# A list scheduler learns that VectorE and ScalarE wait on the result of their direct predecessor

## The chip, the cores and the metric

One core of a Trainium2 chip runs the whole program. The metric is device time in microseconds of one execution. The kernel before the change takes 1433.64 us, the median of three runs (1433.3 to 1433.87). Engines are called by their names in the profile: PE is TensorE's matmul row and PEld its weight loads, DVE is VectorE, ACT is ScalarE, POOL is GpSimd, SP is the queue on which most transfers are issued.

## The reference

Two layers over a sequence of 512 positions, width 1024, all in float32.

- Layer 0: RMSNorm, one input projection, a gated linear recurrence and trailing means, an output projection, residual.
- Layer 1: RMSNorm, a projection of twice the width with a sigmoid gate, a causal convolution of 31 taps per channel, LayerNorm over the channels, swish, a second projection, residual.
- After each: cross-attention with 4 heads into 256 memory tokens, and a gated MLP of inner width 3072 with a causal convolution of 3 taps on its gate branch.

```python
def conformer_conv(x, norm, w1, b1, dw_w, dw_b, ln_g, ln_b, w2, b2):
    h = rms_norm(x, norm) @ w1 + b1
    h = jax.nn.glu(h, axis=-1)
    h = causal_dwconv(h, dw_w, dw_b)
    h = jax.nn.silu(layer_norm(h, ln_g, ln_b))
    return h @ w2 + b2
...
def conv_ffn(x, norm, w_up, dw_w, dw_b, w_down):
    h = rms_norm(x, norm) @ w_up
    g = causal_dwconv(h[..., :D_FF], dw_w, dw_b)
    u = h[..., D_FF:]
    return (jax.nn.gelu(g) * u) @ w_down
```

## The kernel before the change

Channels lie on partitions in tiles of 128, positions along the free dimension. Every float32 operand of a matmul is split into a rounded high half and a low half (`split`: ACT copies the high half, DVE, in places POOL, subtracts it for the low half), and three matmuls stand for one product (`mm3`: high x high, high x low, low x high). Weights come by DMA as `wf` tiles and are split into pairs of `wr` tiles. So each weight costs ACT and DVE one pass each.

Nothing is issued where it is written. A class `Recorder` takes down every operation as a `Node`, then `plan` simulates the five engines and issues the operations in the order of that simulation. All instructions carry the line of the issuing statement in `run` (L498), so places are told by tiles here.

- `cost` gives each node a duration, and `lat`, the time after it until another engine sees its result (PE 0.17, ACT 0.1, DVE 0.08, POOL 0.06 us). `HOP` is 0.04 us on top.
- `late` walks the nodes backwards and gives each a due time, from the due times of its successors.
- The loop in `plan` then picks, on each engine that is free, the ready operation with the smallest rank: the recorded index on PE (within a window of 60 PE nodes), the due time elsewhere. A node becomes ready at `hop(a)` after its last predecessor: for one on the same engine, as soon as the predecessor's duration is over.
- Buffers of the tags `act` and `w` are given out by due time, the others in recorded order.

The chip runs each engine's list strictly in that order, and semaphores see to correctness. Where the simulation believes an engine to be earlier than it is, the real list holds an operation too early, and what stands behind it waits.

Three stages matter below. **The MLP** (`ffn`): per chunk of 128 inner channels, `up` makes seven products of eight matmuls into three PSUM tiles, x in `aux`, w and y in `mm`. ACT copies x out three times and w once (`copy`, tiles `tmp`), and the next product into that tile must wait for the copy. Between the products stand 24 matmuls of `down` for the group before, which have no such wait and serve as cover. **The convolution** (`conformer`): for each of 8 channel tiles, `gated` writes h with one DVE operation, four transfers stack shifted copies of h (tiles `actf`, read by `conv_pe`), PE does the first 8 taps (all taps of the last tile) as matmuls of 32 columns, POOL with ACT does 4, and DVE adds the other 19 one by one into PSUM. **The end of it**: LayerNorm over all eight tiles, then the second projection with weights `pw2`.

## Time and profile before

| | before |
|---|---|
| median of 3 runs | 1433.64 us |
| profiled execution | 1433.83 us |
| its span, first to last instruction | 1432.0 us |
| PE busy | 1421.8 us (99%) |
| weight loads (PEld) | 1199.9 us (84%) |
| DVE busy | 1223.8 us (85%), 1874 instructions |
| ACT busy | 853.2 us (60%) |
| POOL busy | 185.3 us (13%) |
| granted TensorE clock | 1.000 |

The profiled execution takes 1.83 us outside its span, and lies 0.19 us over the median. A row of the timeline gives the start, the duration, engine, line, operation, the tiles written and read, the shape, how many instructions were merged into the row, and in brackets how long the engine had been idle before and what ended that. A row of waits gives an engine and its tile, what it waited for, the total, the count and the longest. Matmul ends are modelled, so a short wait of PE can hide in a busy row.

### The profile page before, as it was taken

The page shows a single profiled execution, that of the slowest core. Times are in us where ns is not written, and L with a number is a line of the kernel's source. Part 1 is how long each engine was busy: PE and PEld are TensorE (multiplying, and loading weights), DVE is VectorE, ACT ScalarE, POOL GpSimd, SP SyncE. Part 2 cuts the span into 40 slices and gives each one's busy share as a digit, 9 for nine tenths or more (in the row PEclk, how much of TensorE's full clock was granted, in tenths as well). Part 3 has the DMA queues.
Part 4 walks back from the last instruction along what each step waited for, and adds up shares of the span by engine and source line. Part 5 has one row for each costly group of instructions (what it writes and reads, how often), then busy time and mean ns, then how long its engine had stood idle before and what let it go on. Part 6 is the DMA issues. An engine that isn't in the chain of part 4 may idle for free. (4 is left out here: it accounts for less than half of the span.)

```text
span 1432.0 us, 20240 instructions
## 1 busy us (share of the span) xinstructions
PE 1421.8 (99%) x7512; PEld 1199.9 (84%) x7512; DVE 1223.8 (85%) x1874; ACT 853.2 (60%) x1298; POOL 185.3 (13%) x196
## 2 busy tenths in 40 slices
PE   9999999999999999999999999999999999999998
PEld 8888888888988888888886676888898888888888
DVE  8986964758999999999967996776699999999996
ACT  8578854446866566656643436654577665666654
POOL 0000000001111010110006663300011111011000
PEclk9999999999999999999999999999999999999999
DMA  9332322228877786886515572322688777787821
GB/s 349 104 103 74 123 96 90 76 86 224 234 205 209 208 215 188 216 211 178 166 57 136 134 230 75 118 84 79 175 230 213 205 192 221 205 222 181 216 90 60
DMA packets 75988, 231.91 MB, mean 162 GB/s; under 512 B 8561, under 2 KB 10609, under 8 KB 75889
## 3 DMA queue, kind: packets, MB, share of 16 engines
q1 hardware_dynamic: 61488, 192.20, 40.7%
q0 software_dynamic: 13824, 37.75, 15.6%
q8 instruction: 59, 0.97, 0.3%
q10 hardware_dynamic: 576, 0.67, 0.1%
q14 instruction: 41, 0.33, 0.1%
HBM read 207.52 MB, written 2.10 MB: 146 GB/s over the span
## 5 line engine op out<-in xcount | busy, mean ns | idle before, releaser
L498 PE MATMUL mm<-act,wr 128*128 128x512 f32 (+1 forms) x4599 | 987.3, 368 | 1.7 <-ACT tmp L498 1.0
L498 PEld LDWEIGHTS mm<-act,wr 128*128 128x128 f32 x4599 | 802.1, 188 | 155.2 <-issue 5.8
L498 ACT ACTIVATE wr<-wf 128x1024 fp32r<-128x1024 f32 x295 | 308.4, 1053 | 116.8 <-PE mm L498 27.0
L498 DVE TENSOR_TENSOR wr<-wf,wr 128x1024 fp32r<-128x1024 f32 x272 | 329.4, 1219 | 37.3 <-ACT wr L498 18.7
L498 PE MATMUL aux<-act,wr 128*128 128x512 f32 (+1 forms) x1509 | 293.7, 337 | 0.1
L498 PEld LDWEIGHTS aux<-act,wr 128*128 128x128 f32 x1509 | 232.6, 190 | 28.8 <-ACT tmp L498 0.5
L498 ACT ACTIVATE tmp<-aux 128x512 f32<-128x512 f32 (+1 forms) x189 | 107.5, 571 | 94.8 <-PE aux L498 93.6
L498 DVE TENSOR_TENSOR tmp<-tmp,tmp 128x512 f32<-128x512 f32 (+1 forms) x151 | 99.4, 658 | 10.1 <-ACT tmp L498 6.3
L498 POOL DMA_DIRECT2D wf<-in_wup x48 | 42.7, 889 | 500.9 <-ACT act L498 275.9
L498 DVE TENSOR_TENSOR x<-x,mm 128x512 f32<-128x512 f32 (+1 forms) x126 | 81.5, 648 | 22.3 <-PE mm L498 21.6
L498 DVE SCALAR_TENSOR_TENSOR aux<-h,par,aux 128x497 f32<-128x497 f32 (+18 forms) x133 | 93.1, 731 | 4.7 <-PE aux L498 2.1
L498 POOL DMA_DIRECT2D wf<-wf x48 | 41.5, 864 | 382.0 <-PE mm L498 129.7
L498 ACT ACTIVATE act<-tmp 128x512 fp32r<-128x512 f32 (+1 forms) x85 | 52.9, 627 | 59.5 <-DVE tmp L498 59.4
L498 ACT ACTIVATE act<-actf 128x512 fp32r<-128x512 f32 (+1 forms) x136 | 70.0, 536 | 28.4 <-DVE actf L498 26.4
L498 PE MATMUL aux<-act,act 128*128 128x256 f32 (+1 forms) x456 | 84.4, 327 | 0.0
L498 PEld LDWEIGHTS aux<-act,act 128*128 128x128 f32 x456 | 73.7, 189 | 11.4 <-ACT tmp L498 0.5
L498 DVE TENSOR_TENSOR act<-actf,act 128x512 fp32r<-128x512 f32 (+1 forms) x136 | 76.0, 583 | 1.7 <-ACT act L498 1.5
L498 DVE SCALAR_TENSOR_TENSOR tmp<-h,par,tmp 128x512 f32<-128x512 f32 x96 | 72.0, 750 | 5.3 <-ACT tmp L498 2.7
L498 ACT ACTIVATE tmp<-h,par 128x512 f32<-128x512 f32 (+3 forms) x69 | 52.6, 782 | 31.2 <-DVE h L498 30.9
L498 POOL TENSOR_TENSOR wr<-wf,wr 128x1024 fp32r<-128x1024 f32 x23 | 55.1, 2406 | 91.2 <-PE mm L498 42.2
L498 DVE TENSOR_TENSOR tmp<-mm,tmp 128x512 f32<-128x512 f32 x84 | 57.1, 685 | 6.4 <-PE mm L498 6.1
L498 DVE TENSOR_TENSOR act<-tmp,act 128x512 fp32r<-128x512 f32 (+1 forms) x85 | 57.6, 682 | 0.4 <-ACT act L498 0.2
(150 smaller groups left out, 1067.2 us busy)
## 6 DMA issues: line engine op xcount, KB each, us to landing
wf<-in_wup SPq DMA_DIRECT2D x144, 512.0 KB, 4.8
wf<-in_wup POOLq DMA_DIRECT2D x48, 512.0 KB, 5.7
wf<-in_wdown SPq DMA_DIRECT2D x48, 512.0 KB, 5.3
actf<-in_wup SPq DMA_DIRECT2D x48, 256.0 KB, 6.3
wf<-wf POOLq DMA_DIRECT2D x48, 256.0 KB, 6.0
wf<-in_pw SPq DMA_DIRECT2D x24, 512.0 KB, 4.0
wf<-in_win SPq DMA_DIRECT2D x20, 512.0 KB, 3.6
wf<-in_wk SPq DMA_DIRECT2D x16, 512.0 KB, 5.9
```

The costliest lines, as they stand in the source:

```text
L498: getattr(eng, method)(*[real(a) for a in args], **{k: real(v) for k, v in how.items()})
```

## The change

The scheduler gets a table `DRAIN` with 0.12 us for DVE and 0.2 us for ACT, and each node a set `feeds`: the later nodes that read what it wrote.

- In the forward simulation, a successor on the same engine that reads the result becomes ready `DRAIN` after the predecessor's duration. Another operation may be put in between. A successor that only overwrites is ready as before.
- In `late`, any successor on the same engine now counts with `DRAIN` and no longer with `HOP` and `lat`. For DVE these are equal (0.04 + 0.08 against 0.12), for ACT 0.14 becomes 0.2, for POOL 0.1 becomes 0, and for PE 0.21 becomes 0. So the due times before a chain of matmuls move too.

No operation is added or removed, except that ACT loads an activation table 32 times and no longer 31. Every operation may be issued at another place. In the two programs' lists, a DVE instruction reads what the DVE instruction just before it wrote 370 times before and 120 times after; among the convolution's taps 73 and 29 times. On ACT it is 24 and 13 times.

```diff
--- before.py
+++ after.py
@@ -185,7 +185,7 @@
     def __init__(self, index, eng):
         self.index, self.eng, self.calls, self.us, self.tail = index, eng, [], 0.0, 0.0
         self.table, self.port, self.lat = None, False, 0.0
-        self.before, self.after = set(), set()
+        self.before, self.after, self.feeds = set(), set(), set()
         self.start = self.end = None
 
 
@@ -206,6 +206,7 @@
     PATIENCE = 40.0
     WIRE = 0.83 / (256 * 1024)
     LAND = {"SP": 1.9, "ACT": 1.9, "POOL": 2.3}
+    DRAIN = {"DVE": 0.12, "ACT": 0.2}
 
     def __init__(self, tc):
         self.tc, self.nc = tc, tc.nc
@@ -260,6 +261,8 @@
         for e in t.writes + (t.reads if write else []):
             if meets(e) and e[3] is not node:
                 node.before.add(e[3])
+                if not write:
+                    e[3].feeds.add(node)
         if write:
             keep = lambda e: not (lo <= e[0] and e[1] <= hi and (e[2] & mask) == e[2])
             t.writes = [e for e in t.writes if keep(e)]
@@ -340,7 +343,10 @@
             for o in reversed(nodes):
                 due = end if o.ideal is None else o.ideal + o.us
                 for a in list(o.after) + extra.get(o, []):
-                    due = min(due, a.due - self.HOP - o.lat - (o.tail + self.LAND[o.eng] + self.SAFE if o.tail else 0.0))
+                    if a.eng == o.eng and not o.tail:
+                        due = min(due, a.due - self.DRAIN.get(o.eng, 0.0))
+                    else:
+                        due = min(due, a.due - self.HOP - o.lat - (o.tail + self.LAND[o.eng] + self.SAFE if o.tail else 0.0))
                 o.due = due - 1.15 * o.us
 
         def turn(t):
@@ -451,7 +457,9 @@
                     del r[i]
                     done += 1
                     heapq.heappush(soon, (o.end, o.index, "end", o))
-                    hop = lambda a: now + us if a.eng == o.eng and not o.tail else o.end + self.HOP
+                    drain = self.DRAIN.get(o.eng, 0.0)
+                    same = lambda a: now + us + (drain if a in o.feeds else 0.0)
+                    hop = lambda a: same(a) if a.eng == o.eng and not o.tail else o.end + self.HOP
                     for a, at in [(a, hop(a)) for a in o.after] + [(a, now) for a in opens.get(o, [])]:
                         wait[a] -= 1
                         a.at = max(getattr(a, "at", 0.0), at)
```

Three places, as the programs hold them. A name such as `tmp_1018_5193` is the kernel's tile `tmp_1018` (the same tile in both) and a number of the build, which says nothing. Before is the fence with L498, the change the one with L506.

ACT in an MLP chunk of layer 0, around the copy of `mm_1015` (the chunk's w, `tmp_1018`). `tmp_1019` is a copy of x, `wr_1052` the high half of a weight of a later `down`, `act_1039` and `act_1066` of later `up` weights, `act_995` of the chunk before's result:

```order
L498 ACTIVATE tmp_1017_5160<-aux_1014_5137 128x512
L498 ACTIVATE act_1039_5162<-actf_1032_5099 128x512
L498 ACTIVATE wr_1052_5172<-wf_1051_5077 128x1024
L498 ACTIVATE act_1066_5179<-actf_1059_5127 128x512
L498 ACTIVATE tmp_1018_5193<-mm_1015_5174 128x512
L498 ACTIVATE tmp_1019_5205<-aux_1014_5137 128x512
L498 ACTIVATE act_1093_5221<-actf_1086_5142 128x512
```

```order
L506 ACTIVATE tmp_1017_5153<-aux_1014_5131 128x512
L506 ACTIVATE act_995_5156<-tmp_994_5090 128x512
L506 ACTIVATE wr_1037_5166<-wf_1030_5016 128x1024
L506 ACTIVATE act_1066_5179<-actf_1059_5118 128x512
L506 ACTIVATE tmp_1018_5186<-mm_1015_5168 128x512
L506 ACTIVATE tmp_1019_5198<-aux_1014_5131 128x512
L506 ACTIVATE wr_1052_5222<-wf_1051_5136 128x1024
```

The split `wr_1052` has moved behind both copies, and `act_995` and `wr_1037`, which were ahead of `tmp_1017`, come behind it.

ACT a chunk earlier, at the copies of `mm_988` and of x (`aux_987`):

```order
L498 ACTIVATE tmp_991_5037<-mm_988_5018 128x512
L498 ACTIVATE tmp_992_5053<-aux_987_4987 128x512
L498 ACTIVATE tmp_993_5079<-aux_987_4987 128x512
L498 ACTIVATE tmp_994_5084<-h2_116,par_129 128x512
L498 ACTIVATE wr_1033_5092<-wf_1031_5045 128x1024
```

```order
L506 ACTIVATE tmp_991_5034<-mm_988_5018 128x512
L506 ACTIVATE wr_1025_5043<-wf_1024_4971 128x1024
L506 ACTIVATE tmp_992_5051<-aux_987_4987 128x512
L506 ACTIVATE wr_1035_5080<-wf_1029_4911 128x1024
L506 ACTIVATE tmp_993_5085<-aux_987_4987 128x512
```

The weight splits `wr_1025` and `wr_1035` have moved ahead of the second and the third copy. On PE three matmuls of `down` (into `mm_1000`) now stand ahead of the product that follows the second copy. The lists show this PE pattern at eight chunks.

DVE in the convolution. `aux_1448` and `aux_1467` are the accumulators of the channel tiles 0 and 1, rows into them are taps, and `h2_116` is the h of channel tile 2:

```order
L498 SCALAR_TENSOR_TENSOR aux_1448_7435<-h0_112,par_129,aux_1448_7435 128x483
L498 SCALAR_TENSOR_TENSOR aux_1448_7435<-h0_112,par_129,aux_1448_7435 128x482
L498 SCALAR_TENSOR_TENSOR aux_1467_7545<-h1_114,par_129,aux_1467_7545 128x500
L498 SCALAR_TENSOR_TENSOR aux_1467_7545<-h1_114,par_129,aux_1467_7545 128x499
L498 SCALAR_TENSOR_TENSOR h2_116<-mm_1468_7514,par_129,tmp_1465_7518 128x512
L498 SCALAR_TENSOR_TENSOR aux_1467_7545<-h1_114,par_129,aux_1467_7545 128x498
L498 SCALAR_TENSOR_TENSOR aux_1467_7545<-h1_114,par_129,aux_1467_7545 128x497
L498 SCALAR_TENSOR_TENSOR aux_1467_7545<-h1_114,par_129,aux_1467_7545 128x496
```

```order
L506 SCALAR_TENSOR_TENSOR aux_1448_7441<-h0_112,par_129,aux_1448_7441 128x488
L506 SCALAR_TENSOR_TENSOR aux_1467_7522<-h1_114,par_129,aux_1467_7522 128x499
L506 SCALAR_TENSOR_TENSOR aux_1448_7441<-h0_112,par_129,aux_1448_7441 128x487
L506 SCALAR_TENSOR_TENSOR aux_1467_7522<-h1_114,par_129,aux_1467_7522 128x498
L506 SCALAR_TENSOR_TENSOR aux_1448_7441<-h0_112,par_129,aux_1448_7441 128x486
L506 SCALAR_TENSOR_TENSOR h2_116<-mm_1468_7507,par_129,tmp_1465_7516 128x512
L506 SCALAR_TENSOR_TENSOR aux_1448_7441<-h0_112,par_129,aux_1448_7441 128x485
L506 SCALAR_TENSOR_TENSOR aux_1467_7522<-h1_114,par_129,aux_1467_7522 128x497
```

Taps of two accumulators now alternate, and the write of `h2_116` has three operations fewer ahead of it since the first tap. The write of channel tile 1's h now stands ahead of all taps. On PE, 6 of the matmuls into `mm_1449` and of those into `mm_1487` move from behind the convolution of channel tile 0 and of tile 2 to ahead of it; of those into `mm_1468`, 12 move the other way at tile 1. Ahead of the tile 4 convolution stand 9 matmuls more, ahead of that of tile 6 another 27 (21 of them 256 wide). At the end of the stage, DVE subtracts the low halves of all three first `pw2` weights (`wr_1672`, `wr_1675`, `wr_1678`) ahead of the second activation's (`act_1632`), which before came behind the first.

## The prediction

> **What bounds the kernel now.** I read the page's busy times first, then the chain of waits, then windows of the long stages, then PE's own waits, then the timeline at the places where it waits.
>
> ```profile
> span 1432.0 us, 20240 instructions
> PE 1421.8 (99%) x7512; PEld 1199.9 (84%) x7512; DVE 1223.8 (85%) x1874; ACT 853.2 (60%) x1298; POOL 185.3 (13%) x196
> ```
>
> PE is busy in all but 10 us. A modelled busy time may hide waits, so I look at its pace. In the chain of waits (start, duration, what):
>
> ```profile
> 1243.86 4.11 PE mm L498 x18
> ...
> 1259.10 4.11 PE mm L498 x18
> ...
> 1274.34 4.11 PE mm L498 x18
> ```
>
> A matmul of 512 columns takes 4.11/18 = 0.228 us, and one MLP chunk follows the other in 15.24 us, twice the same. In the chain itself stands nothing but PE. A faster DVE shortens such a chunk by nothing. Windows of two MLP stretches and of the convolution (PE, PEld, DVE, ACT, POOL busy, clock, DMA):
>
> ```profile
> 480.00:520.00 40.00, 39.94 (x208) 33.91 (x207) 39.19 (x58) 22.40 (x32) 4.90 (x6) 1.00 0.78 214
> 760.00:800.00 40.00, 38.76 (x182) 26.98 (x175) 37.30 (x53) 14.75 (x20) 25.27 (x20) 1.00 0.53 142
> 1200.00:1240.00 40.00, 39.52 (x211) 33.72 (x210) 39.02 (x58) 24.26 (x35) 5.05 (x6) 1.00 0.78 204
> ```
>
> DVE runs at 93 to 98% there, so PE's operands come out of it with little to spare. What can be won is what PE waits. Its waits, of matmuls and of weight loads (total, times, longest):
>
> ```profile
> PE aux L498 <- DMA actf<-h: 1.6, 3, 1.0
> PE mm L498 <- ACT tmp L498: 1.0, 2, 0.5
> PE mm L498 <- DVE act L498: 0.6, 1, 0.6
> ...
> PEld aux L498 <- DMA actf<-h: 5.2, 5, 1.9
> PEld mm L498 <- ACT tmp L498: 4.3, 9, 0.9
> PEld mm L498 <- DVE act L498: 1.2, 2, 0.9
> ```
>
> Two causes stand out: the stacked copies of h in the convolution, and ACT's copies of PSUM in the MLP.
>
> **The price of a dependent neighbour.** Timeline of DVE in the convolution:
>
> ```profile
> 764.33 6.13 DVE L498 SCALAR_TENSOR_TENSOR aux<-h,par,aux 128x497 f32<-128x497 f32 x8
> ...
> 793.36 3.90 DVE L498 SCALAR_TENSOR_TENSOR aux<-h,par,aux 128x484 f32<-128x484 f32 x6
> ```
>
> The first row is eight taps into one accumulator, each reading the one before. At 0.74 us for one, the starts lie (6.13 - 0.74)/7 = 0.77 us apart. The second is six taps that alternate between two accumulators: (3.90 - 0.74)/5 = 0.63. So an operation between two that depend saves 0.14 us. The change puts 0.12. With 370 such neighbours before and 120 after, DVE is relieved of 250 x 0.12 to 250 x 0.14, 30 to 35 us of its 1224. [...]
>
> That relief lies beside PE and is worth nothing by itself. It pays where PE waits.
>
> **Term 1, the convolution.** Timeline of PE, each convolution block (32-column matmuls) and the row that follows it:
>
> ```profile
> 759.14 2.28 PE L498 MATMUL aux<-actf,wf 128*32 128x512 f32 x16
> 761.35 11.19 PE L498 MATMUL mm<-act,wr 128*128 128x512 f32 x48
> 772.47 1.92 PE L498 MATMUL aux<-actf,wf 128*32 128x512 f32 x16
> 774.32 9.86 PE L498 MATMUL mm<-act,wr 128*128 128x512 f32 x42
> 784.10 1.16 PE L498 MATMUL aux<-actf,wf 128*32 128x512 f32 x4
> ...
> 789.38 12.54 PE L498 MATMUL mm<-act,wr 128*128 128x512 f32 x54
> ...
> 814.84 1.06 PE L498 MATMUL aux<-actf,wf 128*32 128x512 f32 x6
> ...
> 818.06 9.83 PE L498 MATMUL mm<-act,wr 128*128 128x512 f32 x42
> ...
> 843.01 2.74 PE L498 MATMUL aux<-actf,wf 128*32 128x512 f32 x16
> 845.68 12.53 PE L498 MATMUL mm<-act,wr 128*128 128x512 f32 x54
> ```
>
> The block of channel tile 1 takes 774.32 - 772.47 = 1.85 us and waits for nothing. Tile 0 takes 2.21, tile 2 5.28, tile 4 3.22, tile 6 2.67. Over 1.85 that is 0.36 + 3.43 + 1.37 + 0.82 = 5.98 us, all of it late copies of h. For tile 2 the cause is on DVE:
>
> ```profile
> 763.66 0.74 DVE L498 SCALAR_TENSOR_TENSOR h<-mm,par,tmp 128x512 f32<-128x512 f32 x1
> ...
> 777.89 0.75 DVE L498 SCALAR_TENSOR_TENSOR h<-mm,par,tmp 128x512 f32<-128x512 f32 x1
> ...
> 778.67 4.26 SPq L498 DMA_DIRECT2D actf<-h  x4
> ```
>
> The product it reads was done six matmuls (1.37 us) after 774.32, at 775.7; DVE came to it 2.2 us later, behind taps. In the new list h comes after 19 operations, 12 of which depend on their neighbour: 0.67 + 12 x 0.77 + 6 x 0.63 = 13.7 us after the first, so near 775.2, and then waits for PE. With 0.3 us from PE's end to DVE's start it can be written 1.9 us earlier. PE also runs six more matmuls, 1.37 us, ahead of the block. Of 3.43 us that takes 1.9 + 1.37 = 3.3. For tiles 0, 4 and 6, PE has 6, 9 and 27 matmuls more ahead of the block: 1.37, 2.05 and at least 3 us, more than the 0.36, 1.37 and 0.82 they wait. Only tile 1 loses: its block comes 12 - 6 = 6 matmuls (1.37) earlier, less the 0.36 saved at tile 0. Its h goes ahead of three taps, 763.66 against 761.46 or so, 2.2 us earlier. Between 0 and 0.9 us could be lost, by what the SP queue does; I take 0.4. Together -(0.36 + 3.3 + 1.37 + 0.82) + 0.4 = -5.4, and I take **-5.0**, since tile 2's transfers took 4.26 us to issue and may again. The bounds are 0 (the transfers alone set it) and -5.98. DVE must follow: 44 fewer dependent taps at 0.14 are 6.2 us, enough.
>
> **Term 2, ACT's copies in the MLP.** Timeline around the longest such wait:
>
> ```profile
> 524.08 1.06 ACT L498 ACTIVATE wr<-wf 128x1024 fp32r<-128x1024 f32 x1 [0.29 <-DVE wr L498]
> ...
> 525.57 0.58 ACT L498 ACTIVATE tmp<-mm 128x512 f32<-128x512 f32 x1
> ...
> 526.20 1.48 PEld L498 LDWEIGHTS mm<-act,wr 128*128 128x128 f32 x8 [0.91 <-ACT tmp L498]
> 526.20 1.69 PE L498 MATMUL mm<-act,wr 128*128 128x512 f32 x8 [0.48 <-ACT tmp L498]
> ```
>
> PE waits for the copy of w; ahead of it ACT split a weight for 1.06 us. The loss is more than the 0.48 shown, since a matmul's row is longer than its pace:
>
> ```profile
> L498 PE MATMUL mm<-act,wr 128*128 128x512 f32 x3639 | 876.9, 391 | 1.7 <-ACT tmp L498 1.0 <-DVE act L498 0.6
> ```
>
> 0.391 - 0.228 = 0.16 is hidden, so 0.64 is lost, 0.27 less than the weight load's 0.91. For the nine such waits: 4.3 - 9 x 0.27 = 1.9 us. In the new list the weight split has gone behind both copies, which takes away 1.06 us where 0.64 was missing. Such a split, needed only much later, was early because ACT was thought idle while DVE ran late. I take **-1.6** of 1.9; bounds 0 and -1.9.
>
> **Term 3, new waits.** Two rows of the lists speak for some. At eight chunks a weight split has moved ahead of a copy of x. Ahead of the second projection, DVE subtracts two more weights before the second activation. The wait already there (0.6 on PE, 0.9 on PEld, both by DVE act) may grow: two splits of 1.2 us go ahead, of which three matmuls each (0.68) cover half, so at most about 1 us more. The other side is that this wait goes, -0.8. I take **+1.3** in all, bounds -0.8 and +2.9 (1 plus as much again as the MLP waits now, 1.9). The additional table load lies on ACT, 60% busy, in a mixer without a PE wait; it counts as nothing, and as its 1.28 us, if it fell in a copy's way:
>
> ```profile
> 1.67 1.28 ACT L498 ACT_TABLE_LOAD   x1 [1.67 <-PEq L1591]
> ```
>
> Sum against the profiled execution: 1433.83 - 5.0 - 1.6 + 1.3 = 1428.5, and the median of the runs lies 0.2 lower. I forecast **1428.4 us**. A measurement here tells from no change what is over 0.2%, 2.9 us, so it counts as faster below 1430.8 and as slower above 1436.5.
>
> **Rivals.**
>
> (a) *The copies of h stay late.* The wait is named as DMA, and the issues of these copies (shortest, median and longest in ns) held one of 2.6 us:
>
> ```profile
> L498 SPq DMA_DIRECT2D actf<-h x28: 548/604/2644, 764.5 to 851.2; - x28
> ```
>
> If the queue sets it, earlier h buys nothing: 1433.8 - 1.6 + 1.3 = 1433.5. Against it: PE also comes later to four of the blocks, whatever the queue does.
>
> (b) *Slower: cover spent too early.* At the eight chunks PE now uses three matmuls (0.68 us) ahead of the product after ACT's second copy of x, because the plan puts a split of
>
> ```profile
> L498 ACT ACTIVATE wr<-wf 128x1024 fp32r<-128x1024 f32 x295 | 308.4, 1053 | 116.8 <-PE mm L498 27.0
> ```
>
> 1.05 us ahead of that copy. If ACT reaches the split late, say behind a DVE result, PE pays up to 1.05 at each: 1428.4 + 8 x 1.05 = 1436.8. It outweighs the gains of 5.3 from 0.66 us a chunk on. For it: ACT waits for DVE often. Against it: ACT is 22 to 24 of 40 us busy here, and the new plan counts the delays on DVE that made ACT late.
>
> (c) *DVE is the bound.* If the stretches at 97% DVE are paced by DVE, 30 us of relief come back whole: 1433.8 - 30 = 1404. Against it: two chunks of exactly 15.24 us, and 0.228 us for each matmul. "Perfetto Trace Analysis" of the Trainium skill, in "Identifying the Most-Contended Engine", would point here: it takes weight-load busy, not matmul busy, as PE's measure, and 84% stands below DVE's 85%. The steady pace disagrees.
>
> (d) *It doesn't do what it says.* The price of a dependent neighbour is not saved, the order moves to no end: about 1433.8. The 0.14 us above are against it.
>
> **Chances.** Forecast 0.61, (a) 0.24, (b) 0.10, (c) 0.02, (d) 0.03. Low end: all of term 1, term 2 and the 0.8 of the wait at the second projection gone, with no new wait, 1433.6 - 6.0 - 1.9 - 0.8 = 1424.9. High end: (a) with the worse half of term 3, 1433.5 + 1 = 1434.5. That leaves out (b) and (c). Faster: the forecast and (c), 0.63, and a bit of (a), 0.02: 0.65. Slower is (b) at its full price, or at half of it together with (a), 1433.5 + 4.2 = 1437.7: 0.10. The rest, 0.25, is the same.
>
> **What would show it.** Term 1: the blocks of tiles 2 and 4 at 1.85 to 2.3 us, the wait for DMA actf<-h on PEld under 1.5 us in all, the row of alternating taps for more than half of the taps. Term 2: PEld's wait for ACT tmp in mm under 2 us. DVE's busy time falls by some 25 to 30 us, as neighbours overlap that did not. Term 3: the wait before the second projection at 0.6 to 1.6 us. If PE waits at eight chunks for ACT tmp after 500 us, (b) was right. If tile 2's block still takes over 4 us, (a). The prediction is wrong at its root if PE's 0.228 us or the 15.24 us a chunk change.

## The result

| | before | after |
|---|---|---|
| median of 6 runs | 1433.46 us (1433.05 to 1433.87) | 1423.87 us (1423.04 to 1425.68) |
| profiled execution | 1433.83 us | 1424.79 us |
| its span | 1432.0 us | 1423.0 us |

The ratio is 0.9934, with a 95% interval of 0.9922 to 0.9947. The change saves 9.6 us, nearly twice the 5.2 us that were forecast, and ends 1 us below the low end of the range. The direction was right, the size was not.

The page of the changed kernel, span and busy times:

```profile
span 1423.0 us, 20230 instructions
...
PE 1414.1 (99%) x7512; PEld 1200.0 (84%) x7512; DVE 1204.5 (85%) x1874; ACT 846.6 (59%) x1299; POOL 185.2 (13%) x196
```

DVE has lost 19.3 us of busy time, PE 7.7, and the span 9.0. The change needs the same 7512 matmuls; what it needs less is waiting. PE's timeline (start, duration) at the convolution blocks of the channel tiles 2 and 4, where before lost most:

```profile
782.55 1.92 PE L506 MATMUL aux<-actf,wf 128*32 128x512 f32 x16
...
810.58 1.92 PE L506 MATMUL aux<-actf,wf 128*32 128x512 f32 x16
```

Both, like those of tiles 0, 1, 3 and 6, are a single row of 16 matmuls with the 1.92 us that the undisturbed tile 1 had before (a start-to-start time of 1.85). Tile 5's row shows 1.89 us, as before. The rows with a bracket for DMA actf<-h are gone: the 5.98 us of the blocks have come back in full. DVE's timeline before, at the stage's first taps and its last merge, and after:

```profile
761.46 2.30 DVE L498 SCALAR_TENSOR_TENSOR aux<-h,par,aux 128x500 f32<-128x500 f32 x3 [2.15 <-PE aux L498]
...
865.63 0.75 DVE L498 SCALAR_TENSOR_TENSOR actf<-aux,par,actf 128x512 f32<-128x512 f32 x1
```

```profile
841.22 9.65 DVE L506 SCALAR_TENSOR_TENSOR aux<-h,par,aux 128x500 f32<-128x500 f32 x15 [0.47 <-PE aux L506]
...
860.30 0.75 DVE L506 SCALAR_TENSOR_TENSOR actf<-aux,par,actf 128x512 f32<-128x512 f32 x1
```

The merge comes 5.33 us earlier. Of this, 1.55 us is a first tap that comes earlier (759.91 against 761.46), and 3.8 us is less time between the two. The first row of the second fence is fifteen taps in a row of alternating accumulators, (9.65 - 0.74)/14 = 0.64 us apart.

The prediction showed three rows of the weight loads' waits (5.2, 4.3 and 1.2). The view of before holds more; without its rows named "issue" and three of 0.3 to 0.4 by DVE, these are:

```profile
PEld aux L498 <- ACT tmp L498: 1.4, 6, 0.4
...
PEld stat L498 <- POOL onesf L573: 1.0, 1, 1.0
PEld mm L498 <- ACT wr L498: 0.8, 1, 0.8
...
PEld aux L498 <- POOL actf L498: 0.7, 2, 0.4
PEld aux L498 <- DVE tmp L498: 0.5, 2, 0.3
```

And the same view after, without "issue" and two rows of 0.4:

```profile
PEld aux L506 <- ACT tmp L506: 1.7, 2, 1.3
PEld aux L506 <- DVE wr L506: 1.3, 1, 1.3
PEld stat L506 <- POOL onesf L581: 1.0, 1, 1.0
PEld mm L506 <- DVE act L506: 0.9, 2, 0.5
```

With all rows but "issue" they add up to 16.1 us before and 5.7 after. The difference of 10.4 us is close to the 9.0 of the span. The rows for DMA actf<-h and for mm <- ACT tmp, 9.5 us, are gone. Two waits are new. The first stands before the second projection (PE's timeline):

```profile
885.88 1.64 PE L506 MATMUL mm<-act,wr 128*128 128x512 f32 x5 [0.19 <-DVE act L506]
...
888.86 0.50 PE L506 MATMUL aux<-act,wr 128*128 128x512 f32 x1 [0.88 <-DVE wr L506]
```

Together 1.07 us where 0.60 stood before. The second was not forecast. It lies in the second MLP's first chunks; ACT's timeline there:

```profile
1051.33 0.63 ACT L506 ACTIVATE act<-actf 128x512 fp32r<-128x512 f32 x1 [1.55 <-DMA actf<-in_wup]
1051.86 1.04 ACT L506 ACTIVATE wr<-wf 128x1024 fp32r<-128x1024 f32 x1
1052.81 0.36 ACT L506 ACTIVATE tmp<-aux 128x256 f32<-128x256 f32 x1
```

ACT waits 1.55 us for a weight to land, and the copy that PE needs stands behind this weight's split and another. PE waits 1.03 us, the weight load 1.34.

Where the 9 us were won shows at rows that stand at the same place of both programs: a row late in the first cross-attention, the first row behind the first MLP, the first behind the second projection, and the start of the output. PE's timeline before, and after:

```profile
317.24 1.03 PE L498 MATMUL aux<-ident,tmp 128*128 128x128 f32 x8
...
725.39 5.92 PE L498 MATMUL mm<-wr,act 128*128 128x256 f32 x48
...
944.44 0.62 PE L498 MATMUL stat<-act,ones 128*128 128x512 f32 x2
...
1423.49 0.71 PE L498 MATMUL aux<-ident,actf 128*128 128x128 f32 x5
```

```profile
316.73 1.04 PE L506 MATMUL aux<-ident,tmp 128*128 128x128 f32 x8
...
722.82 5.92 PE L506 MATMUL mm<-wr,act 128*128 128x256 f32 x48
...
936.44 0.62 PE L506 MATMUL stat<-act,ones 128*128 128x512 f32 x2
...
1414.55 0.71 PE L506 MATMUL aux<-ident,actf 128*128 128x128 f32 x5
```

Ahead of the first MLP 0.5 us are won, in the stretch with the first MLP 2.06, in the one with the convolution and the second projection 5.43, and from there on 0.94, all of it in the second MLP.

### The profile page after: what moved, and what is told of

Same layout as the page of the kernel before. It is cut to its first block, busy times and chain, and to the rows that moved or that the text cites. A ratio compares the mean times of both kernels' runs of the same rounds, so it can differ in the third digit from the quotient of the medians.

```text
span 1423.0 us, 20230 instructions
## 1 busy us (share of the span) xinstructions
PE 1414.1 (99%) x7512; PEld 1200.0 (84%) x7512; DVE 1204.5 (85%) x1874; ACT 846.6 (59%) x1299; POOL 185.2 (13%) x196
## 4 chain that ended last, share of the span: by engine, by line
PE 98%; DMA 1%; DVE 0%; ACT 0%; issue 0%; DVEq 0%; POOL 0%; POOLq 0%
PE mm L506 70%; PE aux L506 27%; PE stat L506 1%; DMA actf<-in_wup 1%; DVE wr L506 0%; ACT wr L506 0%; DVE wf L506 0%; DVEq L1607 0%; ACT act L506 0%; ACT tmp L506 0%; ACT rtok L506 0%; DVE rtok L506 0%; POOL onesf L581 0%; POOL eps L581 0%; DVE act L506 0%
## 5 line engine op out<-in xcount | busy, mean ns | idle before, releaser
L506 PE MATMUL mm<-act,wr 128*128 128x512 f32 (+1 forms) x4599 | 988.0, 368 | 0.2 <-DVE act L506 0.2
L506 PEld LDWEIGHTS mm<-act,wr 128*128 128x128 f32 x4599 | 801.4, 188 | 149.8 <-issue 5.5
L506 ACT ACTIVATE wr<-wf 128x1024 fp32r<-128x1024 f32 x295 | 307.3, 1053 | 105.6 <-PE mm L506 34.8
L506 DVE TENSOR_TENSOR wr<-wf,wr 128x1024 fp32r<-128x1024 f32 x272 | 330.8, 1218 | 39.3 <-ACT wr L506 19.8
L506 PE MATMUL aux<-act,wr 128*128 128x512 f32 (+1 forms) x1509 | 293.6, 336 | 1.9 <-ACT tmp L506 1.0
L506 PEld LDWEIGHTS aux<-act,wr 128*128 128x128 f32 x1509 | 234.0, 190 | 30.6 <-ACT tmp L506 1.3
L506 ACT ACTIVATE tmp<-aux 128x512 f32<-128x512 f32 (+1 forms) x189 | 108.0, 572 | 94.3 <-PE aux L506 91.9
L506 DVE TENSOR_TENSOR tmp<-tmp,tmp 128x512 f32<-128x512 f32 (+1 forms) x151 | 97.8, 647 | 11.6 <-ACT tmp L506 11.0
L506 POOL DMA_DIRECT2D wf<-in_wup x48 | 41.9, 872 | 464.8 <-DMA actf<-in_wup 181.2
L506 DVE TENSOR_TENSOR x<-x,mm 128x512 f32<-128x512 f32 (+1 forms) x126 | 81.4, 646 | 20.6 <-PE mm L506 19.9
L506 POOL DMA_DIRECT2D wf<-wf x48 | 41.3, 861 | 410.4 <-DMA wf<-in_wup 127.0
L506 DVE SCALAR_TENSOR_TENSOR aux<-h,par,aux 128x500 f32<-128x500 f32 (+16 forms) x133 | 89.2, 728 | 3.4 <-PE aux L506 2.3
L506 ACT ACTIVATE act<-tmp 128x512 fp32r<-128x512 f32 (+1 forms) x85 | 52.7, 625 | 58.0 <-DVE tmp L506 57.9
L506 ACT ACTIVATE act<-actf 128x512 fp32r<-128x512 f32 (+1 forms) x136 | 68.8, 534 | 26.7 <-DVE actf L506 19.5
L506 PE MATMUL aux<-act,act 128*128 128x256 f32 (+1 forms) x456 | 84.2, 327 | 0.0
L506 PEld LDWEIGHTS aux<-act,act 128*128 128x128 f32 x456 | 73.8, 189 | 10.9
L506 DVE TENSOR_TENSOR act<-actf,act 128x512 fp32r<-128x512 f32 (+1 forms) x136 | 75.4, 580 | 3.2 <-ACT act L506 3.1
L506 DVE SCALAR_TENSOR_TENSOR tmp<-h,par,tmp 128x512 f32<-128x512 f32 x96 | 71.6, 746 | 0.8 <-ACT tmp L506 0.6
L506 DVE TENSOR_TENSOR tmp<-mm,tmp 128x512 f32<-128x512 f32 x84 | 57.2, 686 | 15.9 <-PE mm L506 15.0
L506 POOL TENSOR_TENSOR wr<-wf,wr 128x1024 fp32r<-128x1024 f32 x23 | 55.2, 2408 | 96.2 <-PE mm L506 53.8
L506 ACT ACTIVATE tmp<-mm 128x512 f32<-128x512 f32 (+1 forms) x58 | 33.3, 574 | 55.7 <-PE mm L506 55.6
L506 ACT ACTIVATE tmp<-h,par 128x512 f32<-128x512 f32 (+3 forms) x69 | 52.4, 778 | 18.0 <-DVE h L506 17.9
```

Source lines behind the costliest of these rows:

```text
L506: getattr(eng, method)(*[real(a) for a in args], **{k: real(v) for k, v in how.items()})
```

## The experiments

All in one view first. The neighbours are the dependent ones of DVE in the program's list; the weight load's waits are the sum of all rows of that view but those named "issue"; DVE busy and span are of the profiled execution.

| kernel | neighbours | PEld waits | DVE busy | span | median | ratio to before, interval |
|---|---|---|---|---|---|---|
| before | 370 | 16.1 | 1223.8 | 1432.0 | 1433.5 | 1 |
| the change | 120 | 5.7 | 1204.5 | 1423.0 | 1423.87 | 0.9934, 0.9922 to 0.9947 |
| forward half alone | 140 | 5.9 | 1205.7 | 1422.5 | 1424.70 | 0.9938, 0.9923 to 0.9953 |
| due times alone | 383 | 13.9 | 1224.7 | 1431.2 | 1433.05 | 0.9998, 0.9989 to 1.0008 |
| VectorE's number alone | 121 | 4.3 | 1206.1 | 1421.8 | 1423.70 | 0.9930, 0.9914 to 0.9947 |
| delay counted, gap not filled | 349 | 8.3 | 1222.2 | 1428.9 | 1429.71 | 0.9976, 0.9966 to 0.9985 |
| convolution alone | 331 | 12.6 | 1219.3 | 1427.2 | 1428.88 | 0.9968, 0.9956 to 0.9980 |
| MLPs alone | 223 | 11.4 | 1212.2 | 1427.5 | 1429.12 | 0.9970, 0.9959 to 0.9981 |
| copies of h counted longer | 372 | 17.7 | 1223.2 | 1432.0 | 1433.75 | 1.0001, 0.9992 to 1.0010 |
| before, a tap less | 385 | 16.8 | 1222.3 | 1434.9 | 1436.05 | 1.0017, 1.0008 to 1.0027 |
| delay counted, a tap less | 350 | 6.0 | 1215.9 | 1423.2 | 1425.15 | 0.9944, 0.9927 to 0.9960 |
| the change, a tap more | 117 | 7.1 | 1211.2 | 1425.7 | 1429.03 | 0.9967, 0.9954 to 0.9980 |
| a third of the numbers | 141 | 3.2 | 1205.7 | 1420.9 | 1422.75 | 0.9925, 0.9909 to 0.9942 |
| a third, VectorE alone | 146 | 4.2 | 1207.3 | 1422.3 | 1422.65 | 0.9926, 0.9909 to 0.9942 |
| twice the numbers | 113 | 7.8 | 1206.5 | 1426.6 | 1428.42 | 0.9965, 0.9952 to 0.9978 |

Each ratio is to before as it ran beside that kernel (medians 1433.32 to 1433.75), over all runs. A difference of the medians in the table can lie up to 0.5 us beside it.

The same by stretch, in us of PE's timeline against before, between rows like those shown above (for the second MLP, from a row late in the second cross-attention on):

| kernel | first MLP | convolution, second projection | second MLP |
|---|---|---|---|
| the change | -2.06 | -5.43 | -0.96 |
| due times alone | -0.28 | -0.04 | -0.50 |
| VectorE's number alone | -2.07 | -5.44 | -2.24 |
| delay counted, gap not filled | -1.18 | +0.54 | -1.74 |
| convolution alone | +0.08 | -4.61 | -0.20 |
| MLPs alone | -2.03 | -0.40 | -2.20 |
| copies of h counted longer | +0.19 | +0.02 | +0.26 |
| before, a tap less | -0.10 | +2.99 | -0.26 |
| delay counted, a tap less | -2.03 | -3.71 | -2.22 |
| the change, a tap more | -2.06 | -1.47 | -2.23 |
| a third of the numbers | -2.09 | -5.95 | -2.26 |
| twice the numbers | -2.04 | -0.44 | -2.21 |

In four of these kernels (gap not filled, before with a tap less, the change with a tap more, twice the numbers) a long wait of PE is followed by a stretch at half of TensorE's clock, which is part of their middle number. The last section has its size.

### Which half

The forward half alone: in `late`, the changed lines give way to the old one.

```diff
-                    if a.eng == o.eng and not o.tail:
-                        due = min(due, a.due - self.DRAIN.get(o.eng, 0.0))
-                    else:
-                        due = min(due, a.due - self.HOP - o.lat - (...))
+                    due = min(due, a.due - self.HOP - o.lat - (...))
```

> Only the forward half of the change: a reader of its direct predecessor's result becomes ready 0.12 or 0.2 us later; the due times are computed as before the change. Theory A (the forward half frees DVE and lets the plan see it truly): nearly the whole gain, 1423 to 1426 us, convolution blocks of 1.85 us. Theory B (the gain comes from the due times, which lost 0.21 us for each step of a chain of matmuls): 1431 to 1434 us. The program's lists hold 140 dependent neighbours on DVE, 35 of them taps (before 370 and 73, after 120 and 29).

The due times alone: the forward simulation forgets the delay.

```diff
-                    same = lambda a: now + us + (drain if a in o.feeds else 0.0)
+                    same = lambda a: now + us
```

> Only the other half: due times as in the change, the forward simulation as before. 383 dependent neighbours on DVE. Theory A: no gain, 1432 to 1436 us, with waits for the copies of h and for ACT's copies as before. Theory B: 1423 to 1427 us.

Measured: 0.9938 and 0.9998. The whole gain is in the forward half; the due times, with all that moved for them on PE and ACT, are worth nothing that can be measured. They do move waits: with them alone, the weight load's wait mm <- ACT tmp falls from 4.3 to 0.9 us and that for DMA actf<-h from 5.2 to 2.8, others grow, and the time stays.

### Which engine

```diff
-    DRAIN = {"DVE": 0.12, "ACT": 0.2}
+    DRAIN = {"DVE": 0.12, "ACT": 0.0}
```

> The change with 0.12 us for DVE and nothing for ACT (32 dependent neighbours on ACT, 121 on DVE). If ACT's part is as small as its 24 neighbours before say (24 x 0.2 = 5 us on an engine that is 60% busy): like the change, 1423 to 1426 us. If ACT's delay is what kept PE's copies late in the MLP: 1426 to 1429 us, with PE waiting for ACT tmp.

Measured: 0.9930, no worse than the change. The number for ScalarE earns nothing that can be measured, and ACT's copies are in time because of VectorE's: the weight load waits for them 0.4 us in all.

### A true plan, or the gap filled

In the change, the planner both learns the true time of a dependent neighbour and puts another operation into the gap. Here it counts the delay as busy time of the engine and issues the reader at once, so its plan is true and no gap is filled.

```diff
+                    b = ran.get(e)
+                    if b is not None and o in b[0].feeds and not b[0].tail:
+                        us += max(0.0, b[1] + self.DRAIN.get(e, 0.0) - now)
+                    ran[e] = o, now + us
                     o.start = now
...
-                    same = lambda a: now + us + (drain if a in o.feeds else 0.0)
+                    same = lambda a: now + us
```

> The change, but the forward simulation does not put other work between two that depend: it issues the reader at once as before, and counts 0.12 or 0.2 us more for it. So the plan knows the delay and DVE still pays it (349 dependent neighbours). Theory A1 (what counts is that DVE is relieved of about 28 us): little gain, 1430 to 1434 us. Theory A2 (what counts is that the plan sees DVE's true times and puts PE's and ACT's work accordingly): most of the gain, 1424 to 1427 us. In the convolution DVE is busy to 97%, so there A1 should hold: its blocks keep 3 us or more of the 6 us of waits. In the MLP A2 should hold: no waits of PE for ACT's copies.

Measured: 0.9976, 3.4 us of the change's 9.6, which lies between the two ranges. PE's timeline at the end of the stage, then DVE's:

```profile
855.28 5.99 PE L510 MATMUL aux<-actf,wf 128*32 128x512 f32 x48 [1.43 <-issue]
...
891.87 0.50 PE L510 MATMUL mm<-act,wr 128*128 128x512 f32 x1 [2.50 <-ACT act L510]
```

```profile
854.43 0.75 DVE L510 SCALAR_TENSOR_TENSOR actf<-aux,par,actf 128x512 f32<-128x512 f32 x1
...
863.74 0.75 DVE L510 SCALAR_TENSOR_TENSOR actf<-aux,par,actf 128x512 f32<-128x512 f32 x1
```

The blocks of channel tiles 0 to 6 take 1.85 to 2.05 us here, so the true plan alone has the copies of h in time. But the last tile's block starts only at 855.28, right behind DVE's merge (854.43 + 0.75 = 855.18; that it waits for the accumulator this merge frees is read from the times, since the profile names no cause), the last merge comes 3.4 us later than in the change, and PE waits 2.50 us ahead of the second projection. DVE, which still has 349 dependent neighbours, ends the stage late. By stretch each theory has its half: the MLPs gain 2.9 us from the true plan alone, where VectorE's number with the gap filled gives 4.3; the convolution with the second projection gains nothing (+0.5), though not at the blocks, where A1 looked for it. Of what is missing there, 1.7 us is the halved clock behind the 2.50 us wait.

### Which stage

The forward half alone, and the delay only for the nodes that one stage records.

```diff
-                    drain = self.DRAIN.get(o.eng, 0.0)
+                    drain = self.DRAIN.get(o.eng, 0.0) if o.stage in ('conv',) else 0.0
```

> The forward half alone, and the delay given only to the instructions that the convolution stage records; those of the two MLPs keep none. Theory (the convolution's 6 us and the MLPs' 3 us are two separate gains with one cause each): the eight channel-tile blocks take 1.85 to 1.95 us each and the wait before the second projection is 1 us, so -6 + 1 there, and the MLPs keep their seven waits of the weight load on tmp: 1427.5 to 1429. Rival (the gain is one thing, VectorE's total busy time): VectorE's dependent neighbours fall only to 331, so the time falls only by the share of neighbours removed, about 50 of 240 of 9 us: 1431 to 1432.

The second kernel has `('mlp',)` there.

> The forward half alone, with the delay given only to the instructions that the two MLPs record; the convolution stage's keep none. Theory of two separate gains: the MLPs' waits on tmp go, worth 2 to 4 us, and the convolution keeps blocks of 2.2 to 5.3 us for four of its tiles: 1429.5 to 1431.5. Rival (VectorE's total): neighbours fall to 223, most of the way, so most of the gain comes with them: 1424 to 1427.

Measured: 4.9 us less and 4.6 us less. They add up to 9.5, against 8.8 to 9.6 for the two stages together. Waits of the weight loads with the convolution alone, and with the MLPs alone:

```profile
PEld mm L504 <- ACT tmp L504: 4.5, 10, 0.9
...
PEld aux L504 <- DMA actf<-h: 0.4, 1, 0.4
```

```profile
PEld aux L504 <- DMA actf<-h: 4.8, 4, 1.9
...
PEld aux L504 <- ACT tmp L504: 0.9, 3, 0.4
```

Each stage heals its own waits and leaves the other's, and by stretch too each gains in its own place. The time of the MLPs alone is 0.4 us below its range. The rival, one gain in proportion to the neighbours removed, is out: the convolution removes 39 of the 250 and gets half of the time.

### The copies of h alone

The planner of before, told that a stacked copy of h lands 2.5 us later than it thought.

```diff
+            node.extra = 2.5 if window else 0.0
...
-                        o.end = wire + self.LAND[o.eng] + self.SAFE
+                        o.end = wire + self.LAND[o.eng] + self.SAFE + o.extra
```

> No delay of a dependent neighbour at all, but the planner counts each stacked copy of h 2.5 us longer than before, so it starts them that much sooner or sends their readers later. Theory A (the blocks wait because the copies of h are planned too tight, whatever the reason): the blocks of channel tiles 0 to 6 take 1.85 to 2.0 us; VectorE's chain is not shortened, so 2 to 4 of the 6 us come back at the stage's end as in the plan that counts the delay without filling it: 1429 to 1432. Theory B (only a VectorE that loses less time can have the copies ready): the blocks of tiles 2 and 4 still exceed 2.3 us, 1432.5 to 1435.

Measured: no gain at all, 1.0001. The time is in theory B's range, but the blocks are as theory A said, and neither theory said where the time would go. PE's timeline:

```profile
787.58 1.92 PE L499 MATMUL aux<-actf,wf 128*32 128x512 f32 x16
...
799.09 1.92 PE L499 MATMUL aux<-actf,wf 128*32 128x512 f32 x16 [1.16 <-issue]
...
828.39 0.62 PE L499 MATMUL stat<-actf,onesf 128*32 128x512 f32 x1 [1.62 <-DVE actf L499]
```

```profile
867.26 0.75 DVE L499 SCALAR_TENSOR_TENSOR actf<-aux,par,actf 128x512 f32<-128x512 f32 x1
```

The blocks are whole, tile 2's 5.28 us included, and the same 6 us stand a few microseconds further on: waits for a merge, for splits, and a last merge 1.6 us later than before. So the late copies of h by themselves are not what the stage loses. That they were where a lag of DVE showed is the reading that fits the runs with the delay; this run does not show it.

### VectorE's load alone, and on a true plan

The kernel before, with the last tap of the convolution left out in seven channel tiles, 5.4 us of DVE.

```diff
-            for i, s in enumerate(range(first + N_POOL[c], TAPS)):
+            for i, s in enumerate(range(first + N_POOL[c], TAPS - 1)):
```

> The kernel before, with the last tap of the convolution left out on VectorE (one instruction less in seven of the eight channel tiles; the convolution then has one tap less there). It relieves VectorE of 7 x 0.77 = 5.4 us in this stage and adds no rule to the planner. Theory A (inside the convolution stage VectorE's chain sets the pace, and the late copies of h are how that shows): 3.5 to 5.5 us of it come back, 1428 to 1430, though all the copies are planned as tight as before. Theory B (the planner's order makes the copies late, and VectorE has time to spare): less than 1.5 us, 1432 to 1434.

Measured: slower, 1.0017, some 2.4 us. PE's timeline, then DVE's and POOL's at the first taps, at the second of these waits and at the last merge:

```profile
821.32 1.05 PE L498 MATMUL stat<-actf,onesf 128*32 128x512 f32 x2 [1.98 <-DVE actf L498]
822.30 5.95 PE L498 MATMUL mm<-act,wr 128*128 128x512 f32 x18
828.18 1.92 PE L498 MATMUL aux<-actf,wf 128*32 128x512 f32 x16
...
861.11 2.90 PE L498 MATMUL mm<-wr,wr 128*128 128x256 f32 x22 [1.46 <-DVE wr L498]
```

```profile
762.67 14.72 DVE L498 SCALAR_TENSOR_TENSOR aux<-h,par,aux 128x500 f32<-128x500 f32 x20 [1.13 <-PE aux L498]
...
855.22 4.75 POOL L498 TENSOR_TENSOR wr<-wf,wr 128x1024 fp32r<-128x1024 f32 x2
...
858.69 2.36 DVE L498 TENSOR_TENSOR wr<-wf,wr 128x1024 fp32r<-128x1024 f32 x1
...
865.55 0.75 DVE L498 SCALAR_TENSOR_TENSOR actf<-aux,par,actf 128x512 f32<-128x512 f32 x1
```

The last merge comes at the same time as before (865.63), though DVE has 5.4 us less to do. One piece of where it went is in the third row: a split that took 1.22 us at this place before took 2.36. It ends 1.08 us after POOL's operation, which runs until 855.22 + 4.75 = 859.97, so it looks held up by POOL; the planner keeps such pairs of DVE and POOL apart in its plan (`port`), and here the real engines had drifted together. The rest are a first tap 1.2 us later (762.67 against 761.46) and more dependent neighbours (385 against 370, among the taps 87 against 73); the sum was not closed. That the kernel is even slower is for the larger part TensorE's clock: behind the 1.98 us wait the 18 matmuls of the next row take 828.18 - 822.30 = 5.88 us, where 18 x 0.228 = 4.10 is usual, 1.8 us lost. So theory A, that DVE's load sets the pace of this stage as it stands, is wrong, and B, which expected next to no change, missed the clock.

The same tap left out on the plan that counts the delay and fills nothing:

> The plan that counts the delay and issues the reader at once, with the convolution's last tap left out on VectorE in seven channel tiles (the convolution has one tap less there). With a true plan alone the blocks took 1.85 to 2.05 us, but VectorE ended the stage 3.4 us later than in the change. Theory A (the change needs both, a plan that is true and 5 us of relief for VectorE): VectorE's last merge moves from 863.7 to 859 to 861, the wait of 2.5 us before the second projection goes, 1423.5 to 1426. Theory B (relief is lost again as it was in the plan of before): VectorE's last merge stays above 862.5, 1428 to 1432.

Measured: 0.9944. DVE's last merge and the longest wait of PE ahead of the second projection:

```profile
858.67 0.75 DVE L510 SCALAR_TENSOR_TENSOR actf<-aux,par,actf 128x512 f32<-128x512 f32 x1
```

```profile
890.46 0.50 PE L510 MATMUL aux<-act,wr 128*128 128x512 f32 x1 [0.89 <-DVE wr L510]
```

Theory A holds, with a merge 0.3 us earlier than its range. The 2.50 us are gone, the merge is 5.1 us earlier than with all taps, and the time falls by 4.6 us. This is not 4.6 us bought with 5.4 us of relief alone: 1.7 us is the halved clock that goes with the wait, and 1.3 us were won in the MLPs. This kernel and the one with a tap less on the old plan do the same work, differ in the planner alone, and lie 0.7% apart, 10 us, of which 1.8 us is the clock and 3.9 us lie in the MLPs. In this one pair, relief paid on the plan that knows the delay and was lost on the one that does not. The change brings both: the truth, and relief from the filled gaps.

The other way round, the change with one tap more for each channel tile, the last one twice:

```diff
-            for i, s in enumerate(range(first + N_POOL[c], TAPS)):
+            for i, s in enumerate([*range(first + N_POOL[c], TAPS), TAPS - 1]):
```

> The change with one more tap of the convolution on VectorE for each channel tile (the last one twice, so the result is that of another filter): 8 x 0.77 = 6.2 us more for VectorE. Theory A (VectorE's chain sets the pace in this stage also after the change): 1427.5 to 1430. Theory B (after the change PE sets it, the blocks waiting for nothing): 1423.5 to 1425.5. Between them, 1425.5 to 1427.5: after the change the two are about level.

Measured: 0.9967 against 0.9934, 4.7 us slower than the change for 6.2 us more of DVE. PE's timeline:

```profile
888.67 0.49 PE L506 MATMUL mm<-act,wr 128*128 128x512 f32 x1 [3.19 <-ACT act L506]
```

The loss stands at the second projection: in the profiled execution the middle stretch is 4.0 us longer than in the change, and 1.6 us of these are the halved clock behind this wait. (The second MLP is 1.3 us shorter, since the change's wait at its start is not there.) The last merge comes at 865.06, 4.8 us later than in the change, so theory A holds in time and in kind. But the order behind the merge has a share: twice the numbers, below, shows the same wait with a merge only 1.1 us later. So the chain of taps has little room in the change; that all of the loss is due to it isn't shown.

### The size of the number

```diff
-    DRAIN = {"DVE": 0.12, "ACT": 0.2}
+    DRAIN = {"DVE": 0.04, "ACT": 0.07}
```

> The change with its two numbers cut to a third (0.04 and 0.07 us). Theory A (most of the gain is from filling the gap, for which any positive number is enough to send another instruction between): dependent neighbours fall about as far (141), 1423.5 to 1426. Theory B (the plan's truth carries it: a third of the number is a third of the lateness cured): 1428 to 1431, with blocks of tiles 2 and 4 above 2.2 us.

Measured: 0.9925, below the range of theory A. Its weight loads wait least of all kernels, 3.2 us, and neither of the two new waits is there.

With 0.04 for VectorE and 0 for ScalarE:

> The change with 0.04 us for VectorE and nothing for ScalarE. If VectorE's number is all that counts and its size does not: 1422 to 1424. If the third was better by chance of order, and the wait before the second projection or the one at the start of the second MLP comes back with ScalarE's number gone: 1424 to 1426.

Measured: 0.9926, as for a number whose size does not count. With the change's numbers doubled, 0.24 and 0.4:

> The change with its numbers doubled (0.24 and 0.4 us). If overstating is harmless, since the number only sends another instruction between: 1423 to 1426. If the plan must be true, VectorE's plan now holds gaps that do not exist, and PE waits where the planner put instructions later than needed: 1426 to 1430.

Measured: 0.9965, in the range of the second theory. It fills as many gaps (113 neighbours left) and is 4.5 us slower than the change, by a row of PE's timeline ahead of the second projection again. ACT's timeline beside it, at the load of the table that the activation ahead of this product needs:

```profile
888.42 0.74 PE L506 MATMUL mm<-act,wr 128*128 128x512 f32 x1 [3.19 <-ACT act L506]
```

```profile
884.79 1.28 ACT L506 ACT_TABLE_LOAD   x1
```

In the change this load starts at 879.79. DVE's last merge is only 1.1 us later (861.37 against 860.30), but in ACT's list splits and copies of weights stand ahead of the load, so most of this wait comes with the order. Behind it the clock is 0.50 for 6.8 us, and 17 matmuls take 6.57 us where 17 x 0.228 = 3.88 is usual: 2.7 of the 4.5 us. A reading that fits, not tested: once gaps are filled, few dependent neighbours are left, so an understated number is seldom wrong, while an overstated one holds readers back. Both thirds are the fastest kernels here, but their intervals overlap that of the change; that they beat it isn't shown.

## Why the prediction was right or wrong

**Term 2, the MLPs, is the step that failed.** It took 1.6 us; the two MLP stretches give 4.2 us in the kernel with the delay in the MLPs alone (2.03 + 2.20), and 4.3 with VectorE's number alone. Some 2.6 us of the 3.7 by which the profiled execution lies below the forecast's sum come from here. Two things in the term were wrong. The first is the loss of a wait, taken at 0.27 us less than the weight load shows. PE's timeline of before at a 0.91 us wait of the other layer, at the chunk's start and the next one's:

```profile
1212.45 4.27 PE L498 MATMUL mm<-act,wr 128*128 128x512 f32 x18
...
1228.44 4.27 PE L498 MATMUL mm<-act,wr 128*128 128x512 f32 x18
```

This chunk takes 15.99 us where an undisturbed one takes 15.24: 0.75 are lost, not 0.64. At 0.16 less than each wait, the nine come to 4.3 - 9 x 0.16 = 2.9 us. The second is that only these nine rows were counted. With the MLPs alone, the two waits for DVE tmp (0.5 us) and 0.5 of the 1.4 us of aux <- ACT tmp go as well; both rows stood in the same view and were taken as nothing. (ACT wr and POOL actf, 1.5 us, stay there and go with the convolution alone.) That leaves between 0.3 and 1.3 of the 4.2 us that are not settled row by row.

Its cause was right in kind: the copies waited because ACT's list was made for a DVE that ran ahead of the real one. VectorE's number alone puts it right.

**Term 1, the convolution, was right in its price and its rows.** The 5.98 us of the blocks went whole, where 5.0 were taken; the 0.4 us for tile 1 and the caution for tile 2's transfers were not needed. Its reason, that h came late because of the taps ahead of it, was only half of the cause: with the copies in time and nothing else, the same 6 us were lost elsewhere. The sentence that DVE must follow, "44 fewer dependent taps at 0.14 are 6.2 us, enough", passed over what turned out to decide: with this relief DVE takes 3.8 us less from its first tap to its last merge, and without it (delay counted, gap not filled) the blocks are as short and the stretch gains nothing.

**Term 3, the new waits,** was taken at +1.3 us and came to some 1.8 (0.55 at the second projection, the 5.98 us less the 5.43 of the stretch, and 1.3 in the second MLP). The one ahead of the second projection came about as sketched, behind the splits for `pw2`, at 0.88 us, and the 0.19 beside it is less than before: 0.47 us more on PE in all. The wait in the second MLP was not foreseen. The kernel without ScalarE's number doesn't have it, nor do the third and twice the numbers, so it is a matter of the order found and not of that number. The 0.5 us ahead of the first MLP were in no term. The additional table load cost nothing that shows.

**The range** did not reach low enough, because its low end summed only the rows that had been made terms. The 16.1 us of all weight-load waits, 15.1 without the one at the start that the change doesn't touch, stood in the view that the terms were taken from and would have given 1433.6 - 15.1 = 1418.5 as the bound.

**The rivals.** (a), late copies whatever the order, is out: no block waits for its transfers. (b), cover spent at eight chunks, did not happen: after 500 us PE waits for ACT tmp once, at 1053, and not there. The chunks keep their pace: two rows of 18 matmuls in PE's timeline after start at 1219.47 and 1234.71, 15.24 us apart as before. (c), DVE as the bound of the whole, is out: it was relieved of 19.3 us and the span of 9.0. By "Identifying the Most-Contended Engine" in "Perfetto Trace Analysis" of the Trainium skill the pick would be DVE, at 85% over 84% of weight loads; the section names MFU, the share of the peak arithmetic, beside the weight loads, which is not worked out here. The steady pace of the chunks speaks against that pick. But in one stage, the end of the convolution, the change leaves DVE close to being the bound, as the tap more showed. (d), that it doesn't do what it says, is out: 250 fewer neighbours relieved DVE of 19.3 us. By "The DRAIN you can't avoid" in "VectorE: DVE Perf Modes" of the Trainium skill the next VectorE operation does not start until the pipe is empty, but one that is not held starts earlier. The trace agrees with the second half: at 0.74 us a tap, alternating taps start every 0.64 us, and taps that read the one before every 0.77. The section gives no price for that difference.

**The signs.** The blocks, the two named waits, the alternating taps, the wait ahead of the second projection and the chunk's pace came out as written. DVE's busy time fell by 19.3 us and not by 25 to 30. The 0.14 us were measured on taps, and part of them was never busy time (a dependent tap is busy for 0.74 of its 0.77 us); over all 250 neighbours it is 19.3/250 = 0.08.

## What to carry to other kernels

Where a planner sets the order of engines that issue strictly in order, first ask whether its durations are true for pairs of instructions, not only for single ones: a wait that shows at one place is often the lag of an engine behind its plan, and mending the place alone can just move it, as with the copies of h. Taking load off that engine paid on the plan that knew the delay and not on the one that didn't, in the one pair tried here. A wait also has to be kept short: behind the longest ones here, TensorE lost another 1.6 to 2.7 us to its clock. To bound such a change, add up every named wait of the engine that sets the pace, not the two rows for which there is a story.

## What was not expected

- A wait costs PE more than its idle time. In before, eight matmuls behind the 0.48 us wait at 526.20 take 1.52 us to the next row, and the same eight without a wait, at 556.83, 1.38.
- Behind a long wait it costs more again. After PE's waits of 1.98 us (before, a tap less), 2.50 (gap not filled) and 3.19 (a tap more) the granted clock is 0.50 for 3.4 us each, and after the other 3.19 (twice the numbers) for 6.8; after 1.62 us (copies of h counted longer) and all shorter waits it stays at 1.00. Stretches of the profiled executions (PE, PEld, DVE, ACT, POOL busy, clock, DMA) with a tap less, with twice the numbers, and behind the 1.62 us wait:

```profile
822.50:825.50 3.00, 3.00 (x8) 2.32 (x9) 2.86 (x5) 0.00 (x0) 2.92 (x3) 0.50 0.79 212
...
889.00:895.00 6.00, 5.40 (x13) 4.14 (x13) 5.97 (x11) 6.00 (x11) 2.38 (x1) 0.50 0.04 14
...
828.50:831.50 3.00, 3.00 (x20) 1.19 (x20) 2.86 (x5) 1.03 (x1) 0.00 (x0) 1.00 0.10 42
```

  By the pace of the matmuls this costs 1.8, 1.7, 1.6 and 2.7 us. So a part of what these four kernels lose is not the order's own, and it differs between executions: the change with a tap more took 1427.4 and 1427.5 us at a mean clock of 0.998, and 1429.0 to 1429.4 at 0.996.
- Seven instructions less on DVE made a kernel 2.4 us slower (1.0017), and one table of the planner moves it by 5.7 us between its third and its double with nearly the same instructions (ACT's table loads differ), the clock's share included. An order that a list scheduler finds is sensitive far from the place of the edit.
- The runs of the change spread over 2.6 us, those of before over 0.8. What makes the difference is open.
